# One flat list of steps in place of nested loops, and another queue for the first load, in a two-layer attention kernel

## The chip, the cores and the metric

The kernel runs on 1 core of one Trainium2 chip. The metric is the time of one execution on the device in microseconds (us), and the time of a kernel is the median of several runs. The core's engines appear in the profile under short names: PE is TensorE's matmul, PEld its weight load, DVE is VectorE, ACT is ScalarE, POOL is GpSimd, SP is SyncE, which here only starts DMA transfers.

## The reference

The reference is a trunk of two layers over x, 512 positions by 1024 channels, all in float32. In each layer one projection of x gives everything else: a latent for queries and one for keys and values, a rotary key, q, k and v of a second attention, and gates. Cut to what matters:

```python
for l in range(DEPTH):                       # 2
    h = x @ w_in[l]
    c_q, c_kv, k_r, gate_a, q_d, k_d, v_d, gate_b, gates = _split_cols(h)
    # branch A: 8 heads; q and k/v come from the RMS-normed latents, rotary key shared by the heads
    o_a = _dense_attention(q_a, k_a, v_a, mla_scale)
    y_a = (o_a * silu(gate_a)) @ w_branch_a[l]
    # branch B: 4 heads, each with two softmax maps
    p = softmax(q_b k_b^T * diff_scale)
    o_b = (p[:, :, 0] - lam * p[:, :, 1]) @ v_b
    o_b = _rms_norm(o_b, g_diff[l], eps=1e-5) * (1.0 - lam_init)
    y_b = (o_b * silu(gate_b)) @ w_branch_b[l]
    g = sigmoid(gates + b_merge[l])
    merged = g[..., :D_MODEL] * y_a + g[..., D_MODEL:] * y_b
    x = _layer_norm(DEEPNORM_ALPHA * x + merged @ w_out[l], ln_gamma[l], ln_beta[l])
return x
```

## The kernel before

**Precision.** Each operand is split into a high part that TensorE takes as is and a low part that holds the rest: ScalarE casts (high), VectorE subtracts (low). A product is then three matmuls, high by high, high by low and low by high (`mm3`, lines 125 to 128). Most matmuls are 128 by 128 weights against 512 columns.

**Stages of a layer.** First come the latents (lines 192 to 250): in layer 0 the eight chunks of x and of the latent weights are loaded, split and multiplied as they come. Then the latents are transposed, the shared rotary key is made, and the values of all eight latent heads (`VS`). The change touches what follows, up to the output projection:

- `keys(c)` (line 300): the keys of heads 2c and 2c+1 into the tiles KE and KO, which all pairs share. `query(h)` (line 309): loads a small weight block on SyncE's queue, splits it, multiplies, applies the rotary table.
- `mla_scores(h)` (line 342): four steps; each multiplies 128 queries with all keys into a `pssc` accumulator, VectorE takes the row maximum (line 172), ScalarE the exponential (line 174).
- `keyT` (line 177): four transposes on TensorE turn the probabilities of 128 keys round into `pstr`; ScalarE casts (line 183) and VectorE subtracts (line 184) to get the high and low part, `pt`.
- `mla_values(h)` (line 356): four steps, each with two matmuls of a `pt` pair into the one `pspv` accumulator, and a fifth that scales by the gate and splits the head pair's result.
- `gateA`, `gate`, `diff_q`, `diff_k`, `diff_v`, and gates of branch B: projections of x. Each takes a 512 KB block from SyncE's queue, is split (lines 112 and 115) and gives 24 matmuls (96 narrower ones for `diff_v`).
- `diff_scores` and `diff_values` (lines 437 and 458): the same for the second attention, with two softmax maps to a step; `diff_values` has six steps, the last two with the per-head norm.
- `branch` and `mergeA` (lines 495 and 514): the branch projections, 12 matmuls for 128 output channels, and the gated merge. The merge of branch B and its gates end the stretch (lines 590 to 601).

**Order.** The loops write the order out: `weave` alternates one score step of head h+1 with one value step of head h, where the value step makes the transposes of the next one; the lists `fill` and `dfill` (lines 557 and 570) say which projections follow which head. After branch A's last head come two projections, then the four score steps of branch B's first head, then its heads with their fills. At the end the gates of branch B come in pairs, followed by the two merges.

**Buffers.** Tiles of one name rotate through a fixed number of buffers (lines 66 and 74): 3 `acc`, 2 `sc`, 2 `tr` and 1 `pv` accumulator, 3 `tmp`, 4 `pt`, 8 `p`, 16 `qm`, 2 `wr` for raw weights and 3 each for their high and low parts. The framework sets the semaphores and decides when a buffer is free.

**The first loads.** Line 121 starts the load of x chunk 0 on ScalarE's queue and those of the other chunks on SyncE's, where the latent weights are loaded too (line 197).

Of the kernel before, what the change touches and what calls it, by code (L numbers as in the profile page):

```python
# [19 lines left out]
SEQ = 512  # L20
# [22 lines left out]
    + [f"o{n}{k}" for n in range(2) for k in range(4)]  # L43
)


# [4 lines left out]
def hybrid_trunk(ctx: ExitStack, tc: tile.TileContext, x, xT, wlat, wts, prm, dlam, gb, tab, rtab, out):  # L51
# [66 lines left out]

    def load_x(k):
        raw = t2("p")  # L120
        (nc.scalar if k == 0 else nc.sync).dma_start(raw, xT[:, k * SEQ:(k + 1) * SEQ])
        nc.scalar.copy(xH[:, k, :], raw)
        nc.vector.tensor_tensor(xL[:, k, :], raw, fr(xH[:, k, :]), ALU.subtract)

# [62 lines left out]
    def layer(l, last):  # L187
# [134 lines left out]
            return split(f, "qm")  # L322


        dlt = t2("tmp")
        nc.sync.dma_start(dlt[:, 0:256], dlam[:, l, :])
        dl = dlt[:, 0:256].rearrange("p (a b c) -> p a b c", a=2, b=2)
        prod = dlt[:, 256:384].rearrange("p (a c) -> p a c", a=2)
        nc.vector.tensor_tensor(prod, dl[:, :, 0, :], dl[:, :, 1, :], ALU.mult)
        ex = small(2)  # L330
        nc.vector.tensor_reduce(ex, prod, axis=AX.X, op=ALU.add)
        nc.scalar.activation(ex, ex, AF.Exp)
        nlam = small(1, "nl", 2)
        nc.vector.scalar_tensor_tensor(nlam, ex[:, 1:2], -LAM_INIT[l], ex[:, 0:1], ALU.add, ALU.subtract)
        gsc = small(1, "gs", 2)
        nc.vector.tensor_scalar(gsc, pr[:, C_GD:C_GD + 1], 0.5 * (1.0 - LAM_INIT[l]), None, ALU.mult)
        bh = small(16, "bh", 2)
        nc.vector.tensor_scalar(bh, pr[:, C_BM:C_BM + 16], 0.5, None, ALU.mult)

        yA, yB, opair = [], [], []  # L340

        def mla_scores(h, q):
            e = h % 2
            KH, KL = KO if e else KE
            if e == 0:
                opair.append((t2("op"), small(8)))
            sums = opair[-1][1].rearrange("p (t e) -> p t e", e=2)
            pts = []
            for t in range(NT):
                S = pt_("sc")  # L350
                tk = slice(t * P, (t + 1) * P)
                mm3(S, q[0][:, tk], q[1][:, tk], KH, KL, True, True)
                pts.append(soft(S, sums[:, t, e:e + 1]))
                yield pts

        def mla_values(h, pts):
            c, e = h // 2, h % 2
            pv = pt_("pv")
            nxt = keyT(pts, 0)
            for kc in range(NT):  # L360
                ph, pl = nxt
                if kc < NT - 1:
                    nxt = keyT(pts, kc + 1)
                v = VS[kc][:, h * P:(h + 1) * P]
                nc.tensor.matmul(pv, lhsT=v, rhs=ph, start=kc == 0, stop=False)  # L365
                nc.tensor.matmul(pv, lhsT=v, rhs=pl, start=False, stop=kc == NT - 1)  # L366
                yield
# [66 lines left out]
                out.append(split(acc, "kv"))  # L434
            return out

        def diff_scores(h, q, k, s1):
            TA, TB = q
            s2 = small(4)
            pts = []  # L440
            for t in range(NT):
                tk = slice(t * P, (t + 1) * P)
                S = pt_("sc")
                nc.tensor.matmul(S, lhsT=TA[:, tk], rhs=k[0], start=True, stop=False)  # L444
                nc.tensor.matmul(S, lhsT=TA[:, tk], rhs=k[1], start=False, stop=True)
                p1 = soft(S, s1[:, t:t + 1])
                S = pt_("sc")
                nc.tensor.matmul(S, lhsT=TB[:, tk], rhs=k[2], start=True, stop=False)  # L448
                nc.tensor.matmul(S, lhsT=TB[:, tk], rhs=k[3], start=False, stop=True)
                p2 = soft(S, s2[:, t:t + 1])  # L450
                cf = small(1)
                nc.vector.reciprocal(cf, s2[:, t:t + 1])
                nc.vector.scalar_tensor_tensor(cf, cf, nlam, s1[:, t:t + 1], ALU.mult, ALU.mult)
                nc.vector.scalar_tensor_tensor(p1, p2, cf, p1, ALU.mult, ALU.add)
                pts.append(p1)
                yield pts

        def diff_values(h, pts, v, g, s1):
            pv = pt_("pv")
            nxt = keyT(pts, 0)  # L460
            for kc in range(NT):
                ph, pl = nxt
                if kc < NT - 1:
                    nxt = keyT(pts, kc + 1)
                o = (kc % 2) * 256 + (h % 2) * P
                vh, vl = v[kc // 2]
                mm3(pv, vh[:, o:o + P], vl[:, o:o + P], ph, pl, kc == 0, kc == NT - 1)
                yield
            o = t2("op")
# [14 lines left out]
            nc.gpsimd.tensor_tensor(r, e, mhalf[:, 0:4], ALU.pow)  # L484
            yield
            b = bcast(r)
            nc.vector.scalar_tensor_tensor(g, b, gsc, g, ALU.mult, ALU.mult)
            nc.vector.tensor_tensor(o, o, g, ALU.mult)
            yB.append(split(o, "lat"))
# [24 lines left out]
        def mergeA(c, th):  # L514
# [3 lines left out]
            m = mA[-1][:, (c % 2) * 512:(c % 2) * 512 + 512]  # L518
            nc.vector.scalar_tensor_tensor(m, th, 1.0, acc, ALU.add, ALU.mult)


        def weave(*gens):

            gens, r = list(gens), None
            first_ = gens[0]
            while gens:
                for g in list(gens):
                    try:
                        v = next(g)
                        r = v if g is first_ else r  # L530
                    except StopIteration:
                        gens.remove(g)
            return r

        qd, kd, vd, gB, hold = {}, {}, {}, {}, {}

        def run(names):
            for f in names:
                i = int(f[-1])
                if f[0] == "a":  # L540
                    gateA(i)
                elif f[0] == "g":
                    hold[i] = gate(0, i)
                elif f[0] == "m":
                    mergeA(i, hold.pop(i))
                elif f[0] == "v":
                    vd[i] = diff_v(i)
                elif f[0] == "b":
                    gB[i] = silu2(proj(l, f"gb{i}"))
                elif f[0] == "q":  # L550
                    qd[i] = diff_q(i)
                elif f[0] == "k":
                    kd[i] = diff_k(i)

        keys(0)
        q = {0: query(0), 1: query(1)}
        fill = {0: ["q0"], 1: ["k0"], 2: [], 3: ["q1"], 4: ["k1", "a2"], 5: [], 6: ["a3"], 7: []}
        ps_ = {0: weave(mla_scores(0, q.pop(0)))}
        for h in range(8):
            if h % 2 == 1 and h < 7:  # L560
                keys(h // 2 + 1)
            if h < 6:
                q[h + 2] = query(h + 2)
            if h < 7:
                ps_[h + 1] = weave(mla_scores(h + 1, q.pop(h + 1)), mla_values(h, ps_.pop(h)))
            else:
                weave(mla_values(h, ps_.pop(h)))
            run(fill[h])
        run(["b0", "v0"])
        dfill = {  # L570
            0: ["g0", "m0", "g1", "m1", "b1", "q2", "k2", "g2", "m2", "g3", "m3"],
            1: ["v1", "b2", "q3", "k3", "g4", "m4", "g5", "m5"],
            2: ["b3", "g6", "m6", "g7", "m7"],
            3: [],
        }
        s1 = {h: small(4, "s1", 3) for h in range(4)}
        ps_ = {0: weave(diff_scores(0, qd.pop(0), kd.pop(0), s1[0]))}
        tail = None
        for h in range(4):
            val = diff_values(h, ps_.pop(h), vd[h // 2], gB[h], s1[h])  # L580
            gens = [diff_scores(h + 1, qd.pop(h + 1), kd.pop(h + 1), s1[h + 1])] if h < 3 else []
            for i in range(5):
                for g in gens:
                    ps_[h + 1] = next(g, ps_.get(h + 1))
                next(val)
                if i == 2 and tail is not None:
                    next(tail)
            tail = val
            run(dfill[h])
        hold["B0"] = gate(1, 0)  # L590
        next(tail)
        merged = []
        for c2 in range(4):
            ths = [gate(1, 2 * c2) if c2 else hold.pop("B0"), gate(1, 2 * c2 + 1)]
            for i in range(2):
                c = 2 * c2 + i
                acc = branch(1, c, yB)
                th = ths[i]
                nc.vector.scalar_tensor_tensor(th, th, 1.0, acc, ALU.add, ALU.mult)
                nc.vector.tensor_tensor(th, th, mA[c // 2][:, i * 512:i * 512 + 512], ALU.add)  # L600
                merged.append(split(th, "qm", 0.5))


        src = x if l == 0 else xs
# [188 lines left out]
```

## Time and profile before

| | us |
|---|---|
| median of 3 runs | 852.66 |
| lowest and highest run | 851.47 and 852.77 |
| the profiled execution | 851.0 |
| its span, first to last instruction | 849.1 |
| PE busy | 837.6 |
| VectorE busy | 587.8 |
| ScalarE busy | 428.0 |

The granted TensorE clock was 0.997 of full speed over the span. Matmuls overlap in the array, so a busy share near 1 doesn't say that TensorE runs at its full rate; the distance from one start to the next does. A matmul row reads: start and length in us, engine, source line, operation, output and inputs by the program's names, shapes, number of instructions. The line of a helper (such as 126 to 128) stands for all its callers, so the names tell the stages apart: `psacc<-xH,wh` is a projection, `pssc` a score, `pstr` a transpose, `pspv` a value product.

### The profile page before, as it was taken

Reading aid. Unit: us, or ns where it says so; the run is one execution under the profiler, and the core shown is the slowest. Engines: PE = TensorE matmul, PEld = TensorE weight load, DVE = VectorE, ACT = ScalarE, POOL = GpSimd, SP = SyncE. Lnnn points to the kernel's source line nnn. Section 1 sums busy time; section 2 is a strip of 40 time slices with the busy share of each in tenths; the row PEclk is TensorE's granted clock in tenths of the full one; section 3 lists DMA queues with packets and bytes.
Section 4 is the critical chain, followed back from the end, with each engine's and each line's share of the span. In section 5 each row is a group of like instructions: output and inputs, shape, how many; then the busy total and the mean of one; then the engine's idle time right before and its main releaser. Section 6 shows DMA issues by size and latency. Waiting matters only on the chain.

```text
span 849.1 us, 11080 instructions
## 1 busy us (share of the span) xinstructions
PE 837.6 (99%) x4143; PEld 695.7 (82%) x4143; DVE 587.8 (69%) x1070; ACT 428.0 (50%) x842; POOL 22.7 (3%) x30
## 2 busy tenths in 40 slices
PE   8999999999999999999999999999999999999996
PEld 7877877878898888888897778788788888888885
DVE  6789988586646845455867899877667566545457
ACT  5767775463544633332336777755546354433310
POOL 0100000000000000000120000000000000000001
PEclk9999999999999999999999999999999999999998
DMA  8311011213222452223532110112222233432322
GB/s 305 118 44 38 32 51 50 74 36 102 87 75 75 124 173 86 93 95 119 185 110 70 39 37 26 50 53 72 76 75 75 79 96 123 155 97 96 100 75 99
DMA packets 27702, 75.70 MB, mean 89 GB/s; under 512 B 3201, under 2 KB 7809, under 8 KB 27649
## 3 DMA queue, kind: packets, MB, share of 16 engines
q1 hardware_dynamic: 27504, 74.74, 27.7%
q8 instruction: 32, 0.52, 0.3%
q10 hardware_dynamic: 144, 0.26, 0.1%
q14 instruction: 22, 0.17, 0.1%
HBM read 70.80 MB, written 4.19 MB: 88 GB/s over the span
## 4 chain that ended last, share of the span: by engine, by line
PE 88%; ACT 5%; DVE 4%; DMA 2%; issue 1%; SPq 0%; POOL 0%; DVEq 0%; ACTq 0%
PE psacc L126 22%; PE psacc L127 22%; PE psacc L128 22%; PE pstr L181 4%; PE pspv L365 2%; PE pssc L126 2%; PE pssc L127 2%; PE pssc L128 2%; PE pspv L126 2%; PE pspv L366 2%; PE pspv L127 1%; PE pspv L128 1%; DMA wr<-in_wts_dram 1%; ACT wh L112 1%; PE pssc L444 1%; PE pssc L448 1%
## 5 line engine op out<-in xcount | busy, mean ns | idle before, releaser
L115 DVE TENSOR_TENSOR wl<-wr,wh 128x512 fp32r<-128x512 f32 x192 | 127.3, 686 | 145.6 <-ACT wh L112 145.2
L126 PE MATMUL psacc<-xH,wh 128*128 128x512 f32 x496 | 195.1, 393 | 0.0
L127 PE MATMUL psacc<-xL,wh 128*128 128x512 f32 x496 | 194.4, 392 | 0.0
L128 PE MATMUL psacc<-xH,wl 128*128 128x512 f32 x496 | 193.9, 391 | 0.0
L112 ACT CAST wh<-wr 128x1024 fp32r<-128x1024 f32 x96 | 101.0, 1052 | 175.0 <-PE psacc L127 115.5
L126 PEld LDWEIGHTS psacc<-xH,wh 128*128 128x128 f32 x496 | 93.2, 188 | 18.9
L127 PEld LDWEIGHTS psacc<-xL,wh 128*128 128x128 f32 x496 | 93.2, 188 | 18.4
L128 PEld LDWEIGHTS psacc<-xH,wl 128*128 128x128 f32 x496 | 93.2, 188 | 18.4
L174 ACT ACTIVATE p<-pssc,sm 128x512 f32<-128x512 f32 x128 | 88.2, 690 | 27.9 <-DVE sm L172 27.4
L172 DVE TENSOR_REDUCE sm<-pssc 128x1 f32<-128x512 f32 x128 | 86.7, 683 | 4.8 <-PE pssc L128 2.4
L183 ACT CAST pt<-pstr 128x512 fp32r<-128x512 f32 x96 | 55.6, 586 | 28.2 <-PE pstr L181 27.9
L184 DVE TENSOR_TENSOR pt<-pstr,pt 128x512 fp32r<-128x512 f32 x96 | 64.7, 685 | 7.1 <-ACT pt L183 6.3
L181 PE MATMUL pstr<-ident,p 128*128 128x128 f32 x384 | 57.3, 272 | 0.1
L181 PEld LDWEIGHTS pstr<-ident,p 128*128 128x128 f32 x384 | 47.3, 140 | 11.8 <-ACT p L174 0.5
L126 PE MATMUL psacc<-wh,xH 128*128 128x256 f32 x128 | 36.3, 284 | 0.0
L127 PE MATMUL psacc<-wl,xH 128*128 128x256 f32 x128 | 36.3, 284 | 0.0
L128 PE MATMUL psacc<-wh,xL 128*128 128x256 f32 x128 | 36.2, 283 | 0.0
L365 PE MATMUL pspv<-pt,vs 128*128 128x512 f32 x64 | 29.1, 455 | 0.4
L126 PE MATMUL pssc<-kv,qm 128*128 128x512 f32 x64 | 26.7, 423 | 0.9 <-ACT kv L306 0.6
L126 PE MATMUL psacc<-y,wh 128*128 128x512 f32 x64 | 25.5, 399 | 0.0
L366 PE MATMUL pspv<-pt,vs 128*128 128x512 f32 x64 | 25.5, 399 | 0.0
L127 PE MATMUL pssc<-kv,qm 128*128 128x512 f32 x64 | 25.3, 396 | 0.0
(296 smaller groups left out, 1591.6 us busy)
## 6 DMA issues: line engine op xcount, KB each, us to landing
wr<-in_wts_dram SPq DMA_DIRECT2D x106, 512.0 KB, 3.6
qr<-in_wts_dram SPq DMA_DIRECT2D x16, 128.0 KB, 2.1
p<-in_gb_dram SPq DMA_DIRECT2D x8, 256.0 KB, 2.9
y<-in_x_dram SPq DMA_DIRECT2D x8, 256.0 KB, 5.3
x_scratch<-y SPq DMA_DIRECT2D x8, 256.0 KB, 2.1
y<-x_scratch SPq DMA_DIRECT2D x8, 256.0 KB, 5.3
out_dram<-y SPq DMA_DIRECT2D x8, 256.0 KB, 2.0
p<-in_xT_dram SPq DMA_DIRECT2D x7, 256.0 KB, 4.9
```

The lines of the kernel that those rows point to most:

```text
L112: nc.scalar.copy(hi, raw)
L115: nc.vector.tensor_tensor(lo[:, c], raw[:, c], fr(hi[:, c]), ALU.subtract)
L126: nc.tensor.matmul(o, lhsT=lh, rhs=rh, start=start, stop=False)
L127: nc.tensor.matmul(o, lhsT=lh, rhs=rl, start=False, stop=False)
L128: nc.tensor.matmul(o, lhsT=ll, rhs=rh, start=False, stop=stop)
L172: nc.vector.tensor_reduce(m, S, axis=AX.X, op=ALU.max, negate=True)
L174: nc.scalar.activation(p, S, AF.Exp, bias=m, scale=1.0, accum_out=sums)
L181: nc.tensor.transpose(b[:, t * P:(t + 1) * P], pts[t][:, c * P:(c + 1) * P], ident)
L183: nc.scalar.copy(h, b)
L184: nc.vector.tensor_tensor(lo, b, fr(h), ALU.subtract)
L365: nc.tensor.matmul(pv, lhsT=v, rhs=ph, start=kc == 0, stop=False)
L366: nc.tensor.matmul(pv, lhsT=v, rhs=pl, start=False, stop=kc == NT - 1)
```

## The change

The steps of a layer between the values of the latent heads and the output projection are written into one list, `STEPS`, of two-character names, and a small table calls the function for each. The transposes (t, T) are steps of their own now, apart from the value steps (v, V), and so are the lambda preparation (L), each gate (g, G) and each merge (m, M). The letters: K keys, Q query, s and S scores of branch A and B, t and T transposes, v and V values, a and b gates of the attention branches, q, k and w the projections of branch B's q, k and v, g and m gate and merge of branch A, G and M those of branch B. Both layers use the same list. The functions themselves compute the same with the same tiles. Apart from that, the first x chunk is loaded from SyncE's queue.

```diff
+STEPS = (
+    "Q0 L0 K0 s0 s0 s0 s0 Q2 Q1 s1 t0 t0 s1 t0 v0 t0 s1 v0 v0 s1 v0 v0 q0 K1 Q3 s2 t1 s2 t1 v1 t1 v1 t1 "
+    "v1 s2 s2 v1 s3 v1 k0 Q4 t2 t2 s3 v2 s3 v2 t2 t2 s3 v2 v2 v2 K2 Q5 t3 t3 s4 v3 s4 s4 t3 v3 s4 t3 v3 "
+    "q1 v3 t4 t4 v4 Q6 v3 v4 t4 t4 s5 v4 v4 s5 s5 Q7 s5 v4 k1 a2 K3 s6 t5 t5 v5 t5 s6 s6 v5 t5 v5 s6 v5 "
+    "v5 t6 s7 t6 t6 s7 v6 s7 s7 t6 v6 v6 v6 a3 t7 t7 S0 S0 t7 v7 t7 v7 v7 v7 v6 w0 v7 b0 b1 S0 S0 S1 S1 "
+    "T0 T0 g1 V0 S1 T0 V0 T0 V0 g0 V0 m0 m1 S1 g2 V0 T1 k2 q2 m2 g3 S2 T1 m3 V1 T1 V1 b2 S2 V0 V1 w1 S2 "
+    "q3 S2 k3 T1 g4 m4 V1 g5 T2 T2 m5 S3 V2 T2 V2 S3 T2 V2 g6 V2 S3 V1 g7 V1 V2 S3 m6 b3 T3 T3 m7 T3 V3 "
+    "V3 T3 G2 G6 V3 V2 V3 V3 G0 V3 G1 M0 G4 M1 G3 M2 M3 G5 M4 M5 M6 G7 M7 "
+)
...
-        (nc.scalar if k == 0 else nc.sync).dma_start(raw, xT[:, k * SEQ:(k + 1) * SEQ])
+        nc.sync.dma_start(raw, xT[:, k * SEQ:(k + 1) * SEQ])
...
-        def mla_values(h, pts):
+        def mla_values(h):
             c, e = h // 2, h % 2
-            pv = pt_("pv")
-            nxt = keyT(pts, 0)
             for kc in range(NT):
-                ph, pl = nxt
-                if kc < NT - 1:
-                    nxt = keyT(pts, kc + 1)
+                if kc == 0:
+                    pv = pt_("pv")
+                ph, pl = keyd[0, h].pop(0)
...
-        def weave(*gens):
...
-        keys(0)
-        q = {0: query(0), 1: query(1)}
-        fill = {0: ["q0"], 1: ["k0"], 2: [], 3: ["q1"], 4: ["k1", "a2"], 5: [], 6: ["a3"], 7: []}
...
+        def lambdas():
+            dlt = t2("tmp")
+            nc.sync.dma_start(dlt[:, 0:256], dlam[:, l, :])
...
+        def merge(c):
+            acc = branch(1, c, yB)
+            th = hold.pop("B%d" % c)
+            nc.vector.scalar_tensor_tensor(th, th, 1.0, acc, ALU.add, ALU.mult)
+            nc.vector.tensor_tensor(th, th, mA[c // 2][:, (c % 2) * 512:(c % 2) * 512 + 512], ALU.add)
+            merged.append(split(th, "qm", 0.5))
+
+        def scores(d, h):
+            if (d, h) not in gens:
+                p = probs[d, h] = []
+                gens[d, h] = diff_scores(h, p, s1[h]) if d else mla_scores(h, p)
+            next(gens[d, h])
+
+        def trans(d, h):
+            k = keyd.setdefault((d, h), [])
+            n = trans_n[d, h] = trans_n.get((d, h), -1) + 1
+            k.append(keyT(probs[d, h], n))
...
+        do = dict(
+            a=gateA, K=keys, L=lambda i: lambdas(),
+            Q=lambda h: qs.__setitem__(h, query(h)),
+            s=lambda h: scores(0, h), t=lambda h: trans(0, h), v=lambda h: values(0, h),
+            S=lambda h: scores(1, h), T=lambda h: trans(1, h), V=lambda h: values(1, h),
+            q=lambda i: qd.__setitem__(i, diff_q(i)), k=lambda i: kd.__setitem__(i, diff_k(i)),
+            w=lambda i: vd.__setitem__(i, diff_v(i)), b=lambda i: gB.__setitem__(i, silu2(proj(l, f"gb{i}"))),
+            g=lambda i: hold.__setitem__(i, gate(0, i)), m=lambda i: mergeA(i, hold.pop(i)),
+            G=lambda i: hold.__setitem__("B%d" % i, gate(1, i)), M=merge)
+        for step in STEPS.split():
+            do[step[0]](int(step[1]))
```

More of the change, by code (lines that the diff above doesn't have):

```diff
@@ L322, in query, with mla_scores @@
             return split(f, "qm")
[L325 to L338, printed above, removed]
         yA, yB, opair = [], [], []
-        def mla_scores(h, q):
-            e = h % 2
+        def mla_scores(h, pts):
+            e, q = h % 2, qs.pop(h)
             KH, KL = KO if e else KE
@@ L347, in mla_scores @@
             sums = opair[-1][1].rearrange("p (t e) -> p t e", e=2)
-            pts = []
             for t in range(NT):
@@ L353, in mla_scores @@
                 pts.append(soft(S, sums[:, t, e:e + 1]))
-                yield pts
-        def mla_values(h, pts):
+                yield
+        def mla_values(h):
             c, e = h // 2, h % 2
-            pv = pt_("pv")
-            nxt = keyT(pts, 0)
             for kc in range(NT):
-                ph, pl = nxt
-                if kc < NT - 1:
-                    nxt = keyT(pts, kc + 1)
+                if kc == 0:
+                    pv = pt_("pv")
+                ph, pl = keyd[0, h].pop(0)
                 v = VS[kc][:, h * P:(h + 1) * P]
@@ L435, in diff_v, with diff_scores @@
             return out
-        def diff_scores(h, q, k, s1):
-            TA, TB = q
+        def diff_scores(h, pts, s1):
+            (TA, TB), k = qd.pop(h), kd.pop(h)
             s2 = small(4)
-            pts = []
             for t in range(NT):
@@ L455, in diff_scores, with diff_values @@
                 pts.append(p1)
[L456 to L460, printed above, removed]
+                yield
+        def diff_values(h, s1):
             for kc in range(NT):
-                ph, pl = nxt
-                if kc < NT - 1:
-                    nxt = keyT(pts, kc + 1)
+                if kc == 0:
+                    pv = pt_("pv")
+                ph, pl = keyd[1, h].pop(0)
                 o = (kc % 2) * 256 + (h % 2) * P
-                vh, vl = v[kc // 2]
+                vh, vl = vd[h // 2][kc // 2]
                 mm3(pv, vh[:, o:o + P], vl[:, o:o + P], ph, pl, kc == 0, kc == NT - 1)
@@ L486, in diff_values @@
             b = bcast(r)
+            g = gB[h]
             nc.vector.scalar_tensor_tensor(g, b, gsc, g, ALU.mult, ALU.mult)
@@ L519, in mergeA @@
             nc.vector.scalar_tensor_tensor(m, th, 1.0, acc, ALU.add, ALU.mult)
-        def weave(*gens):
[L524 to L553, printed above, removed]
@@ L555, in layer @@
-        keys(0)
-        q = {0: query(0), 1: query(1)}
-        fill = {0: ["q0"], 1: ["k0"], 2: [], 3: ["q1"], 4: ["k1", "a2"], 5: [], 6: ["a3"], 7: []}
[L558 to L575, printed above, removed]
-        s1 = {h: small(4, "s1", 3) for h in range(4)}
[L577 to L601, printed above, removed]
+        nlam, gsc, bh = small(1, "nl", 2), small(1, "gs", 2), small(16, "bh", 2)
@@ new lines, in lambdas @@
+        def lambdas():
+            dlt = t2("tmp")
+            nc.sync.dma_start(dlt[:, 0:256], dlam[:, l, :])
+            dl = dlt[:, 0:256].rearrange("p (a b c) -> p a b c", a=2, b=2)
+            prod = dlt[:, 256:384].rearrange("p (a c) -> p a c", a=2)
+            nc.vector.tensor_tensor(prod, dl[:, :, 0, :], dl[:, :, 1, :], ALU.mult)
+            ex = small(2)
+            nc.vector.tensor_reduce(ex, prod, axis=AX.X, op=ALU.add)
+            nc.scalar.activation(ex, ex, AF.Exp)
+            nc.vector.scalar_tensor_tensor(nlam, ex[:, 1:2], -LAM_INIT[l], ex[:, 0:1], ALU.add, ALU.subtract)
+            nc.vector.tensor_scalar(gsc, pr[:, C_GD:C_GD + 1], 0.5 * (1.0 - LAM_INIT[l]), None, ALU.mult)
+            nc.vector.tensor_scalar(bh, pr[:, C_BM:C_BM + 16], 0.5, None, ALU.mult)
@@ new lines, in layer @@
+        qd, kd, vd, gB, hold, qs, gens, probs, keyd, merged = {}, {}, {}, {}, {}, {}, {}, {}, {}, []
+        s1 = {h: small(4, "s1", 3) for h in range(4)}
+        def merge(c):
[9 more added lines that the diff above has]
+            next(gens[d, h])
@@ new lines, in trans, with values @@
+        def trans(d, h):
+            k = keyd.setdefault((d, h), [])
+            n = trans_n[d, h] = trans_n.get((d, h), -1) + 1
+            k.append(keyT(probs[d, h], n))
+        trans_n = {}
+        def values(d, h):
+            if ("v", d, h) not in gens:
+                gens["v", d, h] = diff_values(h, s1[h]) if d else mla_values(h)
+            next(gens["v", d, h])
+        do = dict(
[7 more added lines that the diff above has]
+            G=lambda i: hold.__setitem__("B%d" % i, gate(1, i)), M=merge)
```

## The prediction

> **What bounds the kernel now.** I read the page first: shares of the engines, then the chain of work that ended last.
>
> ```profile
> span 849.1 us, 11080 instructions
> PE 837.6 (99%) x4143; PEld 695.7 (82%) x4143; DVE 587.8 (69%) x1070; ACT 428.0 (50%) x842; POOL 22.7 (3%) x30
> PE 88%; ACT 5%; DVE 4%; DMA 2%; issue 1%; SPq 0%; POOL 0%; DVEq 0%; ACTq 0%
> ```
>
> TensorE (PE) is the bound, and the change takes no matmul away. So the only thing to win is time in which PE runs below its own rate. The busy share hides that, because matmuls overlap: one is 0.39 us long, but the next starts sooner. So I take the rate from stretches of the timeline in which nothing is late (start, length, what).
>
> ```profile
> 350.18 0.39 PE L127 MATMUL psacc<-xL,wh 128*128 128x512 f32 x1
> 352.90 0.39 PE L127 MATMUL psacc<-xL,wh 128*128 128x512 f32 x1
> 314.56 0.60 PE L476 MATMUL pstr<-ident,op 128*128 128x128 f32 x4
> 314.92 0.48 PE L127 MATMUL psacc<-xL,wh 128*128 128x512 f32 x1
> 315.24 0.40 PE L128 MATMUL psacc<-xH,wl 128*128 128x512 f32 x1
> 148.55 0.28 PE L126 MATMUL psacc<-wh,xH 128*128 128x256 f32 x1
> 151.89 0.28 PE L127 MATMUL psacc<-wl,xH 128*128 128x256 f32 x1
> ```
>
> Between the first two rows lie 12 steps: 2.72 / 12 = 0.227 us for a matmul 512 wide. Four transposes with the matmul behind them take 315.24 - 314.56 = 0.68, so the four cost 0.45 beyond its 0.227. Between the last two rows lie 28 steps: 0.119 us for one 256 wide. Now I count what each layer's changed stretch holds, from the windows view: first all of PE, then the transposes alone, then the 256-wide group of the first stretch (three such groups, 64 each; the second stretch has the same).
>
> ```profile
> 44.00:340.00 296.00, 295.30 (x1492) 1.00 0.25 76
> 463.00:755.00 292.00, 291.08 (x1471) 1.00 0.24 75
> ```
> ```profile
> 44.00:340.00 296.00, 35.97 (x240) 1.00 0.25 76
> 463.00:755.00 292.00, 35.98 (x240) 1.00 0.24 75
> ```
> ```profile
> L126 PE MATMUL psacc<-wh,xH 128*128 128x256 f32 x64 | 18.2, 284 | 0.0
> ```
>
> First layer: 1492 - 240 - 192 = 1060 are 512 wide, one of them cut by the window's edge. 1059 x 0.227 + 60 x 0.45 + 192 x 0.119 = 240.1 + 27.0 + 22.9 = 290.0 us, so 6.0 of 296.0 are lost. Second layer: 1038 x 0.227 + 27.0 + 22.9 = 285.2, so 6.8 of 292.0 are lost. (0.2267 unrounded.) **All that a better order can win there is 12.8 us**, 1.5% of the span. The view of waits says where it goes.
>
> ```profile
> PEld pspv L365 <- ACT pt L183: 4.9, 16, 0.6
> PEld pspv L126 <- ACT pt L183: 2.6, 8, 0.5
> ```
> ```profile
> 52.03 0.40 PE L127 MATMUL pssc<-kv,qm 128*128 128x512 f32 x1
> 52.42 0.51 PE L365 MATMUL pspv<-pt,vs 128*128 128x512 f32 x1
> 52.76 0.40 PE L128 MATMUL pssc<-kv,qm 128*128 128x512 f32 x1
> ```
>
> 24 times a value matmul waits for ScalarE's cast of the transposed probabilities. One such wait costs PE what the three timeline rows show: 52.76 - 52.03 = 0.73 where two steps take 0.45, so 0.28 us. 24 x 0.28 = 6.7 us, half of the loss. These rows show something else too: a score matmul, a value matmul, the next score matmul. The code emits the three matmuls of one score together, so something between the code and the chip reorders by readiness. The emitted order is therefore a priority and not the order on the chip.
>
> **The change part by part.** Counted token by token, the list holds the same steps as the loops, 221 of them, each as often as before (this is the whole count; the "190" in the change's few words I don't find). Nothing is added or removed on any engine. Moved work:
>
> *Values further behind their transposes.* I give each step its PE work at the rates above: score step s 3 x 0.227 = 0.68, S 0.91, transposes t and T 0.45, values v 0.45 and V 0.68, a query 1.36, a projection 24 x 0.227 = 5.44, diff_v 96 x 0.119 = 11.4, a branch 2.72. Then I add up what stands between each t and its v. Old: "t0 t0 v0 s1 t0 v0": 0.45 from the first t to its v, 1.6 or 1.1 for the others. New: "t0 t0 s1 t0 v0": 1.6. What v needs is the end of the transposes and the cast:
>
> ```profile
> L181 PE MATMUL pstr<-ident,p x384: 270/272/328, 49.5 to 731.1; 128*128 128x128 f32 x192
> L183 ACT CAST pt<-pstr x96: 572/587/605, 51.8 to 731.4; 128x512 fp32r<-128x512 f32 x96
> L306 ACT ACTIVATE kv<-psacc x16: 577/595/601, 41.2 to 542.1; 64x512 fp32r<-64x512 f32 x16
> L453 DVE SCALAR_TENSOR_TENSOR sm<-sm,nl,s x32: 208/211/223, 164.8 to 710.5; 128x1 f32<-128x1 f32 x32
> ```
>
> 0.27 + 0.59 = 0.86 us. Below that lie, per layer, 9 of 32 distances of the first kind and 5 of 16 of the second (T to V) in the old order: 28 over both layers, close to the 24 waits. In the new list 2 of 32 and 0 of 16, so 4 over both layers; the mean distance goes from 1.1 to 1.8 us and from 1.4 to 7.0. If waits follow the count, 20 of 24 go: -5.7 us. At the other end 0, because the reordering already puts foreign matmuls between, and waits all the same. I take two thirds, -3.8, nearer the count since it foretold the present number well. The stall's next place is the second half of the split on VectorE, which ends 0.69 us after the cast (the row of its kind stands below, L166) and is needed one matmul later.
>
> *Keys with less cover.* K0 had two queries (2.7 us) before its first score, now none; K3 one (1.4), now none; K1 is unchanged, K2 gets 2.3 for 1.4. K3 stalls already (its score is the last row):
>
> ```profile
> 119.32 0.59 ACT L149 ACTIVATE tmp<-psacc 128x512 f32<-128x512 f32 x1
> 119.73 0.40 PE L127 MATMUL psacc<-xL,wh 128*128 128x512 f32 x1
> 120.44 0.73 PE L126 MATMUL pssc<-kv,qm 128*128 128x512 f32 x2 [0.31 <-ACT kv L306]
> ```
>
> 120.44 - 119.73 - 0.227 = 0.48 us, since ScalarE's queue holds the copies of k1 and a gate's tanh (first row) ahead of the key's cast. Upper end: each of four places (K0 and K3 in both layers) grows by one cast and one VectorE pass, 0.6 + 0.7 = 1.3, so +5.2. Lower end 0: projections can fill in, and Q7, moved ahead of k1, leaves the key's cast one less in front. I take a quarter of a cast each, +0.6. Behind a waiting score stand PE's next instructions, all of them, as it runs in order.
>
> *Longer life of the tail's tanh tiles.* G2 and G6 now come before the last value steps and keep two of the three tmp buffers until M2 and M6. The other six gates share the third until M2 is done. An M lets its buffer go after this (L509 is the tanh that waits):
>
> ```profile
> L509 ACT ACTIVATE tmp<-psacc,bh 128x512 f32<-128x512 f32 x32 | 21.9, 684 | 0.1
> L165 ACT ACTIVATE qm<-tmp 128x512 fp32r<-128x512 f32 x16 | 10.1, 632 | 26.3 <-DVE tmp L600 26.3
> L600 DVE TENSOR_TENSOR tmp<-tmp,vs 128x512 f32<-128x512 f32 x16 | 11.1, 692 | 0.6
> L166 DVE SCALAR_TENSOR_TENSOR qm<-tmp,qm 128x512 fp32r<-128x512 f32 x16 | 11.0, 689 | 5.6 <-ACT qm L165 5.6
> L599 DVE SCALAR_TENSOR_TENSOR tmp<-tmp,psacc 128x512 f32<-128x512 f32 x16 | 11.0, 687 | 4.2 <-PE psacc L128 4.2
> ```
>
> 0.39 for the last matmul's end, 0.69 + 0.69 + 0.63 + 0.69 and the next tanh 0.68: 3.8 us, while the gate emitted behind it gives PE 5.44. Cover 1.6 us, cost 0. If it is gone, see the slower rival.
>
> *The lambda step* goes behind query 0 on each queue: one DMA on SyncE and six short VectorE operations. Its result is first used at 164.8 (row L453 above). All of the latent-attention stage covers it: 0; without that cover its one DMA's time, below 1 us.
>
> *The first x chunk.*
>
> ```profile
> 0.73 0.40 ACTq L121 DMA_DIRECT2D p<-in_xT_dram  x1
> 0.74 0.38 SPq L197 DMA_DIRECT2D y<-in_wlat_dram  x1
> 1.18 0.42 SPq L121 DMA_DIRECT2D p<-in_xT_dram  x1
> 4.69 0.38 DVE L201 CAST kv<-y 128x416 fp32r<-128x416 f32 x1 [3.53 <-DMA y<-in_wlat_dram]
> 4.87 1.25 ACT L122 CAST xH<-p 128x512 fp32r<-128x512 f32 x2 [2.42 <-DMA p<-in_xT_dram]
> 5.54 0.46 PE L126 MATMUL psacc<-kv,xH 128*128 128x416 f32 x1 [1.16 <-ACT xH L122]
> ```
>
> SyncE's queue takes 1.18 - 0.74 = 0.44 us an issue. The first weight chunk moves from 0.74 to about 1.18, so its cast from 4.69 to 5.13, ending 5.51; the first matmul needs that and the first of the two x casts, which ends at 4.87 + 1.25 / 2 = 5.49 if x lands as now. Start of PE: +0.0 to +0.44; I take +0.3, since the low half of the weights, needed by the second matmul, is later by the full 0.44. All later chunks are issued 0.44 later, hidden by the matmuls of the chunks before. The Trainium skill, page "DMA: Bandwidth & Descriptors", section "Issuing engines are not separate DMA queues", speaks against this edit: a second issuing engine saves the sequencer's issue time, and only that. By the rule alone this part would cost the whole issue, 0.44 for 0.3; no run here shows it yet.
>
> Another sentence of the skill bears on the headroom: "Perfetto Trace Analysis", section "Identifying the Most-Contended Engine", calls matmul busy time a bad measure and points to the weight loads' share. By that, 18% of the span, some 153 us, would be free; the trace disagrees, as a stretch without any wait shows 83% too.
>
> ```profile
> 340.00:372.00 32.00, 32.00 (x143) 26.51 (x142) 15.53 (x24) 11.18 (x14) 0.00 (x0) 1.00 0.29 91
> ```
>
> (26.51 / 32.00 = 0.83, and 142 weight loads.)
>
> **Sum:** -3.8 + 0.6 + 0 + 0 + 0.3 = -2.9 us. The profiled span 849.1 becomes 846.2, its execution 851.0 becomes 848.1. The runs' median is 852.66, so 1.7 above the profiled execution; the median to expect is **849.8**. By the bounds alone this case runs from 852.66 - 5.7 = 847.0 to 852.66 + 5.2 + 0.44 = 858.3; its own range is 846.5 to 852.
>
> **Rivals.**
> *The reordering washes it out* (the list doesn't do what it says): matmuls go by readiness, as the rows at 52.03 show, and the waits come from casts later than whatever placed them thought. Then there are new waits of the same size in other places and +0.3 at the start: 853.0. For it: the list's "t0 t0 v0" had two score matmuls in between and still waited. Against: the count of short distances fits that of the waits.
>
> *The tail turns slower.* If the reordering hands the third tmp buffer to a later gate first (G4 ahead of G1, say), G1's tanh waits for M2, its accumulator stays taken, and with three psacc buffers PE stops until an M's evacuation is through: 3.8 us less the cover that is left. It decides once a tanh is held back longer than the 5.44 us of matmuls behind it. One such stop a layer, 2 x 3.8 = 7.6, against the -2.9: 857.4. For it: only 1.6 us of slack, and two buffers held for over 30 us of PE work. Against: the merge steps are ready work that PE can take first.
>
> *Nearly all of the loss goes*: the softmax steps, spread over the gates, also remove the waits for p and keys: 12.8 less what is lost to entering and leaving each stretch, some 3 us: -9.8 + 0.3, 843.2. For it: the new distances are long nearly everywhere. Against: VectorE has little left in the first stage, 51.5 of 56 us, whatever the order.
>
> ```profile
> 44.00:100.00 56.00, 55.89 (x278) 44.46 (x277) 51.52 (x91) 40.80 (x87) 0.00 (x0) 1.00 0.14 43
> ```
>
> **How the numbers follow.** Gain as summed 0.47, washed out 0.24, slower tail 0.20, nearly all 0.09. A measurement here tells a change from none from about 0.2%, 1.7 us, so faster is below 850.95 and slower above 854.4. The first case is faster but for 0.05 that fall within; the second gives 0.20 same, 0.02 to each side; the third is slower but for 0.01 within. Faster 0.42 + 0.02 + 0.09 = 0.53, same 0.05 + 0.20 + 0.01 = 0.26, slower 0.19 + 0.02 = 0.21. The range runs from just above the best case to just short of the slow tail: 844.0 to 857.0.
>
> **What would show it.** Right: the waits of value matmuls for L183's cast fall from 24 to 10 or fewer, PE matmuls per stretch stay the same, the first matmul starts at 5.5 to 6.0, gates' tanh in the tail never hold up PE. Wrong: as many waits as now under other names, key casts (L306) with over 1 us each, or a gap of PE in the tail with a psacc buffer waiting for a tanh. A loss outside the two stretches would show that I looked in the wrong place.

## The result and the profile after

The changed kernel takes 844.74 us (median, 844.14 to 845.39), the kernel before on the same chip 852.07 (850.87 to 852.77): a ratio of 0.9916, with a 95% interval of 0.9898 to 0.9933. So it is **7.3 us faster**, where 2.9 were forecast. The profiled execution took 844.14 us. First the page of the changed kernel: span, busy shares, chain.

```profile
span 842.4 us, 11052 instructions
PE 831.9 (99%) x4143; PEld 697.4 (83%) x4143; DVE 587.9 (70%) x1070; ACT 426.9 (51%) x842; POOL 22.8 (3%) x30
PE 92%; DVE 3%; ACT 2%; DMA 2%; issue 0%; SPq 0%; POOL 0%; DVEq 0%; ACTq 0%
```

The number of matmuls and VectorE's time are as before; in the chain of work that ended last PE's share went from 88 to 92%. The windows view of the changed kernel, for all of PE and then for the transposes alone, answers the prediction's four rows.

```profile
44.00:340.00 296.00, 295.62 (x1505) 1.00 0.24 76
463.00:755.00 292.00, 291.60 (x1488) 1.00 0.24 76
...
44.00:340.00 296.00, 36.11 (x240) 1.00 0.24 76
463.00:755.00 292.00, 36.11 (x240) 1.00 0.24 76
```

In the same time PE does 13 matmuls more in the first layer and 17 more in the second, with the same transposes. At 0.227 us each that is 6.8 us of the 12.8 that the prediction counted as lost. The view of waits shows which went. These are the changed kernel's (line numbers are 14 higher in most places: L197 was L183, L361 was L365, L188 was L174, L320 was L306; us in total, times, longest), and then the rows of the kernel before that the prediction did not show.

```profile
PEld pspv L361 <- ACT pt L197: 2.4, 6, 0.8
PEld pspv L362 <- DVE pt L198: 0.9, 2, 0.5
PEld pssc L439 <- ACT p L188: 0.6, 2, 0.3
PEld pssc L140 <- ACT kv L320: 0.5, 2, 0.3
PEld pssc L140 <- ACT p L188: 0.5, 3, 0.2
```
```profile
PEld pssc L126 <- ACT p L174: 2.0, 7, 0.6
PEld pssc L126 <- ACT kv L306: 1.5, 2, 0.8
PEld pspv L366 <- DVE pt L184: 1.3, 6, 0.2
PEld pssc L444 <- ACT p L174: 1.2, 6, 0.3
```

Value matmuls waited 24 times for ScalarE's cast, 7.5 us in all; now it is 6 times, 2.4 us. The waits of score matmuls for ScalarE's exponential (`p`), which reads their accumulator, fall from 3.2 to 1.1 us, those for the keys from 1.5 to 0.5. (These are waits of weight loads, which overlap the matmul ahead; the three sums together fall by 8.2 us, the time in these stretches by 6.8.)

**A yardstick.** The first matmul of the output projection is the same work in both layers and in every order, and so is all that lies between the two. These are its timeline rows in the kernel before and in the changed one.

```profile
378.51 0.39 PE L126 MATMUL psacc<-wh,qm 128*128 128x512 f32 x1
798.22 0.39 PE L126 MATMUL psacc<-wh,qm 128*128 128x512 f32 x1
```
```profile
375.34 0.39 PE L140 MATMUL psacc<-wh,qm 128*128 128x512 f32 x1
791.44 0.39 PE L140 MATMUL psacc<-wh,qm 128*128 128x512 f32 x1
421.02 0.35 PE L142 MATMUL psacc<-kv,xL 128*128 128x416 f32 x1
424.98 0.35 PE L142 MATMUL psacc<-qw,xL 128*128 128x416 f32 x1
```

The stretch takes 419.71 before and 416.10 after: 3.6 us less. Behind it the kernels are alike (849.1 - 798.22 = 50.9 and 842.4 - 791.44 = 51.0). Its work at PE's own rates is 1496 matmuls 512 wide, 288 transposes, 192 matmuls 256 wide and 96 of 416 wide (the last two rows: 21 steps in 3.96 us, 0.188 each): 339.1 + 32.4 + 22.9 + 18.1 = 412.5 us. The rest of a stretch is its **loss**: 7.2 before, 3.6 after. Counted the same way, from layer 1's first score to the last value matmul of branch A (called A below) it is 4.2 before and 2.5 after, from there to the output projection (B) 2.3 and 0.8. The other 0.4 us of the gain lies ahead of the first score, 0.7 before and 0.3 after; the new list has the first query ahead of the first keys there, and no run moved that alone.

### The profile page after: what moved, and what is told of

Same layout as the page of the kernel before. It is cut to its first block, busy times and chain, and to the rows that moved or that the text cites. A ratio compares the mean times of both kernels' runs of the same rounds, so it can differ in the third digit from the quotient of the medians.

```text
span 842.4 us, 11052 instructions
## 1 busy us (share of the span) xinstructions
PE 831.9 (99%) x4143; PEld 697.4 (83%) x4143; DVE 587.9 (70%) x1070; ACT 426.9 (51%) x842; POOL 22.8 (3%) x30
## 4 chain that ended last, share of the span: by engine, by line
PE 92%; DVE 3%; ACT 2%; DMA 2%; issue 0%; SPq 0%; POOL 0%; DVEq 0%; ACTq 0%
PE psacc L141 23%; PE psacc L142 23%; PE psacc L140 23%; PE pstr L195 5%; PE pssc L140 2%; PE pssc L141 2%; PE pssc L142 2%; PE pspv L361 2%; PE pspv L362 2%; PE pspv L142 2%; PE pspv L140 2%; PE pspv L141 2%; DMA wr<-in_wts_dram 1%; PE pssc L439 1%; PE pssc L443 1%; PE pssc L444 1%
## 5 line engine op out<-in xcount | busy, mean ns | idle before, releaser
L188 ACT ACTIVATE p<-pssc,sm 128x512 f32<-128x512 f32 x128 | 87.6, 688 | 36.2 <-DVE sm L186 35.8
L198 DVE TENSOR_TENSOR pt<-pstr,pt 128x512 fp32r<-128x512 f32 x96 | 65.0, 682 | 1.5 <-ACT pt L197 0.6
L197 ACT CAST pt<-pstr 128x512 fp32r<-128x512 f32 x96 | 55.2, 586 | 13.5 <-PE pstr L195 10.9
L361 PE MATMUL pspv<-pt,vs 128*128 128x512 f32 x64 | 27.3, 426 | 0.6 <-ACT pt L197 0.6
L140 PE MATMUL pssc<-kv,qm 128*128 128x512 f32 x64 | 26.5, 419 | 0.0
L179 ACT ACTIVATE qm<-tmp 128x512 fp32r<-128x512 f32 x16 | 10.1, 633 | 31.7 <-DVE tmp L538 31.7
```

Of the source, the lines that this page charges most:

```text
L140: nc.tensor.matmul(o, lhsT=lh, rhs=rh, start=start, stop=False)
L188: nc.scalar.activation(p, S, AF.Exp, bias=m, scale=1.0, accum_out=sums)
L197: nc.scalar.copy(h, b)
L198: nc.vector.tensor_tensor(lo, b, fr(h), ALU.subtract)
```

## The experiments

One table for all; the text below says what each kernel is. The ratio is to the kernel before on the same chip. "Cast waits" are those of value matmuls for ScalarE's cast, times and us, in both layers.

| kernel | median us | ratio, 95% interval | stretch | loss | A | B | cast waits |
|---|---|---|---|---|---|---|---|
| before | 852.07 | | 419.71 | 7.2 | 4.2 | 2.3 | 24, 7.5 |
| after | 844.74 | 0.9916 [0.9898, 0.9933] | 416.10 | 3.6 | 2.5 | 0.8 | 6, 2.4 |
| x0_sync | 852.21 | 0.9996 [0.9987, 1.0005] | 419.72 | 7.2 | 4.1 | 2.3 | 24, 7.5 |
| list_alone | 845.04 | 0.9910 [0.9896, 0.9923] | 415.93 | 3.4 | 2.4 | 0.8 | 6, 2.4 |
| first_half | 847.82 | 0.9944 [0.9931, 0.9958] | 417.69 | 5.2 | 2.6 | 2.3 | 14, 5.0 |
| second_half | 849.53 | 0.9963 [0.9949, 0.9976] | 418.32 | 5.8 | 4.2 | 0.8 | 17, 4.8 |
| t_before_v | 856.70 | 1.0053 [1.0038, 1.0068] | 422.57 | 10.1 | 6.9 | 2.4 | 9, 2.7 |
| new_near | 852.05 | 1.0005 [0.9995, 1.0014] | 419.93 | 7.4 | 5.1 | 2.2 | 26, 8.1 |
| lambda_first | 843.85 | 0.9905 [0.9885, 0.9925] | 416.04 | 3.5 | 2.5 | 0.7 | 6, 2.4 |
| keys_covered | 848.22 | 0.9953 [0.9937, 0.9969] | 417.70 | 5.2 | 4.2 | 0.7 | 5, 2.3 |
| no_wl_old | 852.23 | 1.0002 [0.9991, 1.0012] | 419.97 | 7.5 | 4.1 | 2.8 | 30, 7.7 |
| no_wl_new | 847.38 | 0.9937 [0.9917, 0.9957] | 417.83 | 5.3 | 4.0 | 0.8 | 10, 2.6 |
| q7_late | 847.52 | 0.9939 [0.9919, 0.9959] | 417.77 | 5.3 | 4.3 | 0.8 | 4, 2.2 |
| k0_late | 847.66 | 0.9941 [0.9925, 0.9958] | 417.75 | 5.3 | 4.3 | 0.8 | 10, 2.3 |

The kernel before and x0_sync run the same order, and their stretches differ by 0.01 us. So differences of some tenths mean something there. The time ahead of the stretch differs by 1.2 us between the same two traces (378.51 and 379.71), and the runs of one kernel by up to 2.1 us.

### Which part of the change: x0_sync, list_alone, first_half, second_half

All four use the list and its table. Lines with a minus are the changed kernel's, unless a comment says otherwise. **x0_sync** has the order of the nested loops written as a list, with the first x chunk on SyncE's queue:

```diff
-    "Q0 L0 K0 s0 s0 s0 s0 Q2 Q1 s1 t0 t0 s1 t0 v0 t0 s1 v0 v0 s1 v0 v0
...
+    "L0 K0 Q0 Q1 s0 s0 s0 s0 Q2 s1 t0 t0 v0 s1 t0 v0 s1 t0 v0 s1 v0 v0
...
```

> The order of before, written as a list (every engine gets the instructions of before in the order of before), with only the first x chunk moved to SyncE's queue. My prediction's term: +0.3 us, first x matmul at 5.5 to 6.0. The rival, that two queues loading at once slow each other's first landing (in the changed kernel the first weight chunk landed 2.55 us after its issue, before 3.95): first x matmul at about 5.05, time 0.3 to 0.5 us shorter.

**list_alone** has the new order with the chunk on ScalarE's queue, as before; the next two have that queue too.

```diff
-        nc.sync.dma_start(raw, xT[:, k * SEQ:(k + 1) * SEQ])
+        (nc.scalar if k == 0 else nc.sync).dma_start(raw, xT[:, k * SEQ:(k + 1) * SEQ])
```

> The new list, but the first x chunk stays on ScalarE's queue. If the parts add up and the load gains what the traces' first scores show (44.12 against 43.77): 0.35 us longer than the changed kernel, so about 845.1, and 24 waits of value matmuls for the cast of the probabilities down to 6. If my +0.3 for the load were right: 0.3 shorter than the changed kernel.

**first_half** takes the new list up to a3 and the old order behind it; **second_half** the other way round.

```diff
 # first_half, the list from a3 on
-    a3 t7 t7 S0 S0 t7 v7 t7 v7 v7 v7 v6 w0 v7 b0 b1 S0 S0 S1 S1 T0 T0 g1 V0
+    a3 v6 t7 t7 v7 t7 v7 t7 v7 v7 v7 b0 w0 S0 S0 S0 S0 S1 T0 T0 V0 S1 T0 V0
...
 # second_half, the list up to a3
-    "Q0 L0 K0 s0 s0 s0 s0 Q2 Q1 s1 t0 t0 s1 t0 v0 t0 s1 v0 v0 s1 v0 v0
+    "L0 K0 Q0 Q1 s0 s0 s0 s0 Q2 s1 t0 t0 v0 s1 t0 v0 s1 t0 v0 s1 v0 v0
...
```

> New list up to a3 (branch A's heads), old order behind it, first x chunk on ScalarE's queue. Waits by distance: in the compiled order of TensorE the first value matmul stands less than 1.2 us of PE work behind its transposes 34 times in before, 6 times in the changed kernel, 26 times here. If the loss goes with that count, 5.7 us for 28: -1.6 in the two stretches, -0.7 before layer 1's first query, so about 2.3 us under before. Rival, that branch A is where PE loses most (5.1 of 7.3 us a layer) and so gains most whatever the distances: -4 or more.

> Old order up to a3, new list behind it, first x chunk on ScalarE's queue. By the count of short distances (16 of 34 left): -3.7 us against before, none of it before layer 1's first query. Rival, that the gain sits in branch A: -1 to -2.

The chunk's queue alone gives 0.9996, which holds 1: no effect that can be told. The list alone gives all of the gain, 0.9910. Its halves nearly add up: 2.0 us a stretch from the first, 1.4 from the second, 3.4 of the 3.8 of list_alone; and each acts where it was changed, since A falls in one and B in the other. The count of short distances, by which I expected 2.3 us from the first half and 3.7 from the second, does not foretell this: over the whole kernel the first gives 4.9, as its rival had it, and the second 3.1.

### Is it the distance of the values? t_before_v, new_near

The prediction's main step says that a wait goes when v stands further behind its t. **t_before_v** is the old order with the steps of a head's round shifted against each other: the first transpose stands ahead of the round's first score step, and the first three value steps stand one score step later, for branch B likewise. So the distance grows and all other steps keep their places. **new_near** is the new list with each t and T moved back to just ahead of its v or V, score steps and all else staying.

```diff
 # t_before_v, against the old order
-    s1 t0 t0 v0 s1 t0 v0 s1 t0 v0 s1 v0 v0
+    t0 s1 t0 s1 t0 v0 s1 t0 v0 s1 v0 v0 v0
...
 # new_near, against the new list
-    s1 t0 t0 s1 t0 v0 t0 s1 v0 v0 s1 v0 v0
+    s1 s1 t0 t0 v0 s1 t0 v0 t0 v0 s1 v0 v0
...
```

> The order of before in everything but the score, transpose and value steps of one head's round, which go 't s t s t v s t v s v v v' instead of 's t t v s t v s t v s v v' (both branches; first x chunk on ScalarE's queue, as in before). Short distances between transposes and values in the compiled order: 16 instead of 34 (6 in the changed kernel). Yardstick: from the first matmul of the output projection of layer 0 to that of layer 1, 419.71 us in before and 419.72 in the run with the old order as a list, 415.92 with the new list. If distance is what counts, in proportion: -3.8 x 18 / 28 = -2.4 there. Rival, that the spreading of scores, projections and merges over each other gives the gain: 0 to -0.8.

> The new list, but each transpose step moved back to stand before its value step as in the loops (t t v, t v, t v, v); all other steps keep their order. 22 short distances. By distance: the stretch between the two output projections 3.8 x 16 / 28 = 2.2 us longer than with the new list, 418.1, and some 16 waits for the cast. Rival, the spreading: as with the new list, 415.9 to 416.7.

In t_before_v most cast waits go, 24 to 9. But the kernel is **slower** than before, 1.0053. Its view of waits shows what took their place (the last two rows are the cast waits that are left):

```profile
PEld pssc L140 <- ACT p L188: 3.4, 9, 0.9
PEld psacc L140 <- DVE tmp L335: 3.2, 2, 1.6
PEld pstr L195 <- DVE pt L198: 2.8, 9, 0.5
PEld pspv L362 <- DVE pt L198: 2.6, 12, 0.3
PEld pspv L140 <- ACT pt L197: 1.6, 4, 0.5
PEld pspv L361 <- ACT pt L197: 1.1, 5, 0.3
```

The score matmuls now wait 3.4 us for p in this row alone (2.0 before), the transposes for VectorE to free their accumulator (`pstr` to be read at L198), the value matmuls for VectorE's half of the split, 12 times for 6, and a projection stands 1.6 us a layer for an accumulator that VectorE's L335 still reads. In layer 1 this stall is followed by a stretch at a lower clock, which costs 1.5 us; without that A would be 5.4, still above 4.2. The stall itself costs 1.5 of it (both are worked out in the last section); without it too A would be 3.9, near the 4.2 of before. So in A this one stall makes the kernel slower, and no run shows whether it belongs to the longer distance or to this order alone. Apart from it the longer distance gains next to nothing. In new_near the waits for the cast are all back, and so is the whole loss; those for p have grown from 3.2 to 7.0 us:

```profile
PEld pspv L361 <- ACT pt L197: 4.7, 18, 0.5
PEld pssc L140 <- ACT p L188: 4.3, 16, 0.4
PEld pspv L140 <- ACT pt L197: 3.4, 8, 0.5
PEld pssc L439 <- ACT p L188: 2.7, 8, 0.5
```

So with the distance short or long, and all else old or new, there are four kernels. B loses 2.3 (short, old), 2.4 (long, old), 2.2 (short, new) and 0.8 (long, new); A 4.2, 5.4 after the correction for the clock, 5.1 and 2.5. **Neither the longer distance nor the rest of the new order gives anything by itself here; together they give all.** The idea that each wait taken away is worth 0.28 us wherever the rest stands has fallen. One reading is that a tile transposed earlier needs other ready work in the meantime, here the score and gate steps that the new list puts there. No run shows this directly, and t_before_v makes the distance in one way only, mostly by later values.

### Is it VectorE's load? no_wl_old, no_wl_new

A rival: the waits exist because VectorE is nearly full in A, and the new list only spreads its work. Both kernels leave out the low-part pass of the projections' weights on VectorE and multiply a constant zero tile in its place, so PE's work stays; one has the old order, the other the new list.

```diff
-        for i in range(0, 1024, 512):
-            c = slice(i, i + 512)
-            nc.vector.tensor_tensor(lo[:, c], raw[:, c], fr(hi[:, c]), ALU.subtract)
-        return hi, lo
+        return hi, lz
```

> The order of before (first x chunk from SyncE), with VectorE's two passes for the low part of a projection's or branch's weights left out and one constant tile multiplied in their place; TensorE and ScalarE do what they did. Between the output projections PE loses 7.2 us with the old order and 3.6 with the new one (time less matmuls at their own rate). Theory VectorE: waits come from VectorE's queue being nearly full in the rounds, so the old order's loss falls below 4 us. Theory distance: the value matmuls wait for ScalarE's cast 0.59 us long, whatever VectorE does; some 20 of those waits and over 6 us of loss stay.

> The same left out of the new list. Theory VectorE: its loss hardly falls (3.6 to about 3), so that the gap to the old order without these passes is under 1 us. Theory distance: a gap of about 3.6 us stays.

The windows view over layer 1's branch A shows VectorE relieved (behind the length stand PE, PEld, VectorE): 123.31 us of 146 in the kernel before and 110.02 in no_wl_old. Over branch B it falls from 106 us of 186 to 71 of 187.

```profile
466.00:612.00 146.00, 145.30 (x752) 118.14 (x751) 123.31 (x222) 97.47 (x205) 1.01 (x1) 1.00 0.16 48
```
```profile
466.00:612.00 146.00, 145.81 (x752) 117.79 (x751) 110.02 (x198) 97.02 (x205) 1.01 (x1) 1.00 0.14 45
```

PE does the same 752 matmuls in it, the loss stays at 7.5, and there are 30 cast waits in place of 24. So with 13 us less of VectorE's work in A and 35 less in B the old order's waits stay, and this rival falls. The new list keeps its B (0.8 against 2.8) but loses its advantage in A (4.0 against 4.1). So the gap between the two orders is 2.1 us, which neither theory foretold (under 1, and 3.6): in A the gain hangs on details, as the next runs show.

### The keys and the lambda step: keys_covered, lambda_first, q7_late, k0_late

**lambda_first** puts the lambda step ahead of query 0, so that its load is issued first. **keys_covered** gives K0 and K3 the query behind them that covered them in the old order. **q7_late** is the second of these two moves alone. **k0_late** is an attempt at a better list: lambda_first, and the projection k0 behind two transposes.

```diff
 # lambda_first
-    "Q0 L0 K0 s0
+    "L0 Q0 K0 s0
 # keys_covered: both; q7_late: the second only
-    "Q0 L0 K0 s0 s0 s0 s0 Q2 Q1
+    "Q0 L0 K0 Q1 s0 s0 s0 s0 Q2
-    s5 s5 Q7 s5 v4 k1 a2 K3
+    s5 s5 s5 v4 k1 a2 K3 Q7
 # k0_late, with lambda_first
-    k0 Q4 t2 t2 s3
+    Q4 t2 t2 k0 s3
```

> The new list, beginning with L0 Q0 K0 in place of Q0 L0 K0. My prediction's term: 0. Rival, that ScalarE's queue waited in before for the lambda's load, ahead of the first query's casts (a wait of PE's weight load behind the lambda's exponential, 0.7 us in layer 1): 0.7 us longer between the output projections.

> The new list with the cover of the old order behind the keys: Q1 between K0 and the first score, Q7 behind K3 instead of ahead of k1. My prediction's term, +0.6 for both layers, would give 0.3 us less between the output projections. Rival, that PE fills the place anyway and ScalarE's queue is what delays the key's cast: 0, or longer by up to 0.5 a layer, since Q7's cast then stands in that queue again.

> The new list with Q7 behind K3 again, as in the old order, and Q1 left where the new list has it. The run with both moved back lost 1.7 us in branch A of layer 1 (4.22 us of loss against 2.52). If the late query in ScalarE's and VectorE's queues, behind k1 and the gate, is the cause: 1.4 to 1.7 of it here. If the first key's cover is: under 0.4.

> An attempt at a better list: the lambda first as in the run before (843.85 us), and k0 behind the two transposes that follow it, so that its six ScalarE copies no longer stand ahead of the cast that the value matmul at 500.3 us waits for (0.49 us, with 0.11 behind it, in both layers). If nothing else moves: 1.2 us less than that run, 842.7. Rival, that the copies then delay the next scores: 0 or longer.

lambda_first's stretch is 416.04 against 416.10: the lambda step costs nothing at its place. Its ratio, 0.9905, cannot be told from that of the changed kernel.

keys_covered is slower than the changed kernel by 1.6 us a stretch, all in A, and q7_late alone by 1.7. So Q7's move carries that loss, and K0's cover changes nothing. My term for the covers gave 0.3 us the other way. In the new order Q7 stands ahead of k1, a2 and K3, and in q7_late behind them. Its view of waits has a new row, and the timeline at the place shows the wait (bracket: idle time ahead, and what ended it).

```profile
PEld pspv L361 <- issue: 1.2, 2, 0.6
```
```profile
520.61 0.69 DVE L402 SCALAR_TENSOR_TENSOR qm<-tmp,qm 64x512 fp32r<-64x512 f32 x1
...
521.31 0.69 DVE L177 TENSOR_TENSOR qm<-tmp,qm 128x512 fp32r<-128x512 f32 x1
...
522.01 0.69 DVE L368 TENSOR_TENSOR op<-pspv,tmp 64x512 f32<-64x512 f32 x1
...
522.25 0.39 PE L141 MATMUL psacc<-xL,wh 128*128 128x512 f32 x1
...
522.86 0.47 PE L361 MATMUL pspv<-pt,vs 128*128 128x512 f32 x1 [0.21 <-DVE op L368]
```

On VectorE L368, which reads the one `pspv` accumulator of the finished head, comes behind L402 and L177, low parts of two queries, back to back. The next head's first value matmul waits for it. This costs 522.86 - 522.25 - 0.227 = 0.38 us of the 1.7; the rest is spread over A, and no run places it. k0_late, from which I had hoped for 1.2 us, loses the same 1.7 in A, with 10 cast waits against 6. It leaves Q7 where the new list has it and still shows the same wait for L368 (0.22 us of idle PE at 522.23), so the place of Q7 is not all that brings it. **B's gain is there in every kernel that has the new second half unmoved (0.7 to 0.8); A's is lost by either of two small moves.** Why A ends near 4.2 each time is open.

### The start

The timeline's first rows of the changed kernel, then of list_alone, in which only the queue of the first chunk differs:

```profile
0.74 0.39 SPq L211 DMA_DIRECT2D y<-in_wlat_dram  x1
1.18 0.89 SPq L135 DMA_DIRECT2D p<-in_xT_dram  x2
...
3.29 0.38 DVE L215 CAST kv<-y 128x416 fp32r<-128x416 f32 x1 [2.13 <-DMA y<-in_wlat_dram]
...
5.05 0.46 PE L140 MATMUL psacc<-kv,xH 128*128 128x416 f32 x1 [0.66 <-ACT xH L136]
...
22.40 0.62 ACT L176 CAST p<-wr 128x512 fp32r<-128x512 f32 x1 [4.00 <-DMA wr<-in_wts_dram]
...
30.41 0.62 PE L282 MATMUL pstr<-ident,tmp 128*64 128x128 f32 x4 [0.85 <-DVE tmp L279]
```
```profile
4.82 0.38 DVE L215 CAST kv<-y 128x416 fp32r<-128x416 f32 x1 [3.66 <-DMA y<-in_wlat_dram]
...
20.95 0.62 ACT L176 CAST p<-wr 128x512 fp32r<-128x512 f32 x1 [3.28 <-DMA wr<-in_wts_dram]
```

SyncE issues the weights first (0.74), not x. The first weight chunk is there at 3.29 instead of 4.82 (4.69 in the kernel before), and PE starts at 5.05 against 5.54 before; in all nine traces with one queue it starts at 4.71 to 5.05, in the five with two at 5.38 to 5.67. Part of this goes again: a later block's cast (L176), for which ScalarE's queue stands still, comes at 22.40 against 20.95 and 21.95, and at 30 us PE waits for a chain behind it. In x0_sync the cast comes at 22.90, and that wait is longer:

```profile
22.90 0.62 ACT L176 CAST p<-wr 128x512 fp32r<-128x512 f32 x1 [4.08 <-DMA wr<-in_wts_dram]
...
30.91 0.63 PE L282 MATMUL pstr<-ident,tmp 128*64 128x128 f32 x4 [1.23 <-DVE tmp L279]
```

That the late cast makes the wait at 30 us is read from the order of ScalarE's queue; no run moved the one without the other. The first score starts at 43.77 us in the changed kernel and at 44.64 in list_alone, but at 45.15 in x0_sync and at 44.12 before, one trace each. So what the earlier start is worth by then stays open; over the whole kernel x0_sync shows nothing.

## Why the prediction was right or wrong

**Where the loss lies: right.** PE's own rates gave 12.8 us to win in the two stretches, and 6.8 of them came back there, nearly all of the 7.3.

**Values further behind their transposes: right on the waits, wrong on what they are worth.** I took -3.8, two thirds of the count's -5.7. The cast waits fell by 5.1 us, from 24 to 6 (10 or fewer were to show it right). They go roughly by the distance: 9 are left in t_before_v, 26 come back in new_near. But the step's price, 0.28 us for each wait taken away, falls with t_before_v, which lost 15 of the 24 and gained next to nothing in A, its stall left out, and nothing in B. The gain needs both, the distance and the rest of the new order, so no run gives this term a size of its own.

**The stall's next place: counted at nothing, and a gain.** The sum had no term for the softmax steps; they stood in the rival in which nearly all loss goes. The waits of scores for p fell by 2.1 us, those for VectorE's half from 1.3 to 0.9. The sum lacked this and the next point; these are sums of waits, and no run prices them apart from the others.

**Keys with less cover: wrong sign.** I added 0.6 by counting only the query behind the keys. The waits for keys fell from 1.5 to 0.5 us. K0's lost cover cost nothing that a run can tell, and Q7's earlier place, which I had noted as a mere reason for the lower end, is worth 1.7 us a stretch in the new list, as q7_late shows; only part of that through K3's own wait.

**The lambda step and the tanh tiles: right.** lambda_first differs by 0.06 us in the stretch. My bound for a load without cover, below 1 us, was too low: in the kernel before it lands 3.9 us after its issue. B, which holds the tail, loses 0.8 in all, so the two held tmp buffers stop nothing; the slower rival (857.4) did not come about.

**The first x chunk: wrong order of issue, wrong sign at the start.** I moved the weight chunk to 1.18 and PE's start by +0.3; the weights kept 0.74 and PE started 0.5 earlier. Over the whole kernel the effect cannot be told from zero (x0_sync). The rule of the Trainium skill that I weighed there ("DMA: Bandwidth & Descriptors", section "Issuing engines are not separate DMA queues": a second engine saves issue time only) would have cost 0.44; the trace does not bear out that price, since with one queue the first chunk landed sooner.

**The rivals.** "Washed out" has its truth in new_near and t_before_v, where the waits come back under other names, but not for the change as a whole. "Nearly all of the loss goes" (843.2, chance 0.09) came nearest to the measured 844.74; I held VectorE's load against it, and no_wl_old speaks against the load as the reason for the waits. The measured time lies below 847.0, the least that the sum's own bounds allowed. So the direction was foretold by the sum, but the size was not: it lies in the range only because this rival had stretched it down to 844.0.

## What to carry to other kernels

When PE is the bound, measure its loss against its own step time in each stretch, and price a reordering by that and not by the count of one kind of wait: a wait taken away alone can come back under another name. Here a longer distance between producer and consumer paid only together with the rest of the new order. Test the halves and each move of a new order by themselves, since some gains stay under every variation (B here) and others are lost by moving one step (A).

## What the runs showed of the hardware

In t_before_v the same stall of PE occurs in both layers, with different sequels. The timeline of layer 0 and of layer 1, and the windows view (last but two: granted clock):

```profile
120.39 1.04 PE L195 MATMUL pstr<-ident,p 128*128 128x128 f32 x8
122.79 0.50 PE L140 MATMUL psacc<-xH,wh 128*128 128x512 f32 x1 [1.36 <-DVE tmp L335]
...
126.10 0.39 PE L141 MATMUL psacc<-xL,wh 128*128 128x512 f32 x1
...
541.42 1.03 PE L195 MATMUL pstr<-ident,p 128*128 128x128 f32 x8
543.83 0.50 PE L140 MATMUL psacc<-xH,wh 128*128 128x512 f32 x1 [1.37 <-DVE tmp L335]
...
546.13 0.63 PE L140 MATMUL psacc<-xH,wh 128*128 128x512 f32 x1
546.55 0.63 PE L141 MATMUL pssc<-kv,qm 128*128 128x512 f32 x1
...
548.67 0.40 PE L141 MATMUL psacc<-xL,wh 128*128 128x512 f32 x1
```
```profile
122.00:129.00 7.00, 5.84 (x28) 1.00 0.22 75
...
543.00:550.00 7.00, 5.82 (x19) 0.76 0.20 75
```

The eight transposes ahead of the stall take 2 x 0.45 = 0.90 us, so it costs 122.79 - 120.39 - 0.90 = 1.5 us in layer 0 and 543.83 - 541.42 - 0.90 = 1.5 in layer 1. After 1.36 us of idle PE the clock stays at 1.00 in layer 0. After 1.37 us it falls to a mean of 0.76 in layer 1, with steps of 0.42 us in place of 0.227, and the same matmuls take 548.67 - 543.83 = 4.84 us against 126.10 - 122.79 = 3.31: 1.5 us more. The Trainium skill, page "TensorE: Matmul & The Clock Gate", section "Why this matters for your kernels", warns of idle gaps above some 3 us; here a shorter gap was followed by a lower clock once in two times, in the one execution that was traced.

The other thing is the start: with two queues issuing at once the first weight chunk was ready later, at 4.54 to 4.82 us in the five traces with two queues and at 3.21 to 3.35 in the nine with one, though it was issued at the same 0.74 us in all.
